# Last output product of a Strassen-form encoder layer: its weights loaded earlier and split earlier, its row statistics begun earlier

## Chip, cores and metric

The kernel runs on one core of a Trainium2 chip. The metric is device time in microseconds (us). The kernel before has a median of 2124.32 us over three runs (2120.95 to 2125.03).

## The reference

One layer of a hybrid encoder on a sequence of 1024 rows and 2048 columns. Attention and pooling branches give `merged` (1024 x 2048). The part that the change touches is the end:

```python
    merged = g_a * (y_a @ w_br_attn) + g_p * (y_p @ w_br_pool)
    o = merged @ w_out
    return x + gate[:, None] * rmsnorm(o, post_g)
```

`rmsnorm` divides each row of `o` by the root of the mean of its squares, so a row of the output can be written only when all 2048 columns of `o` in that row are known. Everything is in 32-bit floats.

## The kernel before

**Arithmetic.** A product of 32-bit floats is made from two reduced-precision parts: `split` (L95) copies a tile into a high part on ScalarE (L96, `hi`) and subtracts it from the source on VectorE (L97, `lo`). Three matmuls (hi by hi, lo by hi, hi by lo; L1351 to L1353 in the output stage) stand for one. The large products use the Strassen-Winograd scheme: seven block products in place of eight, of sums and differences of blocks. The sums of blocks of `w_out` (S1 to S4) are computed earlier in the program and lie in DRAM as `ws_d`; the blocks themselves (A11, A12, A22) are read from `w_out`.

**The output stage.** `out_pair(half, i, ...)` computes, for one half of the rows in each Strassen block and one half of the columns in each block, four result blocks. It runs four times; the last call (half 1, i 1) is called the final pair here. A call makes seven products in this order, each of 8 steps `j` for two row tiles `t`, that is 48 matmuls into PSUM banks X, Z or V. They are numbered 1 to 7 here; the code counts them from 0 (`n`):

1. A11 by B11 into X, which is then copied to Z
2. S3 by T3 into V, copied to `p7`
3. S2 by T2 added to Z, copied to `u2`
4. A12 by B21 added to X, which gives result block 11 (`c11`)
5. A22 by T4 added to V, with `u2` gives block 21
6. S1 by T1 added to Z, copied to `u4`, with `p7` gives block 22
7. S4 by B22 added to Z, which gives block 12 (`c12`)

`split_weights` (L1399) loads the raw weights of a product in four transfers of 512 KB (tag `raw`, ring of four buffers, tile name `wr`) and splits them step by step into a ring of four `whi` and four `wlo`. `between(n, jp)` is called after every second step of product n+1 and issues side work: for the final pair it is `between_11` (L1564). The prepared operands (B11, T3, ... B22, tiles `mh` and `ml`) fill the pool `big`, a ring of 56 slots of 256 KB; a new tile takes the slots in the order in which they were first given, so it must wait until the matmuls that read the old operand are done.

**Product 7 of the final pair** is written apart (L1470 to L1493). In the kernel before its weights are split ahead into 16 slots of `big` (`ring=False`), but the raw tiles come through the same ring of four as all the others, so their four transfers of 512 KB are issued behind those of product 6. Product 7 runs all 24 matmuls of row tile t=0 first and then those of t=1.

**Rows and their scale.** `result` (L1436) squares a block on ScalarE and sums along the row into `ssq[:, T, n]` (L1361), and multiplies it by the gain `g` on VectorE (L1441). `row_scale` (L1363) sums the four numbers (L1365), takes the root on ScalarE (L1366) and the reciprocal (L1367). `finish_block` (L1370) computes `r * scale + x` on VectorE (L1372) and stores it; the rows of x come as tiles `xr` (`fetch_x_block`, 256 KB each, into slots of `big`). Row tiles T=4 and 5 are finished by `third_block` (after product 5 they have all they need), row tile 6 after the t=0 half of product 7, and row tile 7 after the t=1 half.

**What sets the order.** Every engine executes its own list in order. A scheduler places the instructions in these lists; `keep` (L91) pins an instruction where the program puts it. All loads and the last stores go through SyncE's (SP's) list and its one queue; the stores of the first rows go through GpSimd's (POOL's).

Of the kernel before, what the change touches and what calls it, by code (L numbers as in the profile page):

```python
# [13 lines left out]
F32 = mybir.dt.float32  # L14
F32R = mybir.dt.float32r
AF = mybir.ActivationFunctionType
ALU = mybir.AluOpType
AX = mybir.AxisListType
# [3 lines left out]
P = 128  # L22
S = 1024
D = 2048
# [7 lines left out]
EPS = 1e-6  # L32
# [11 lines left out]
def encoder_layer(ctx: ExitStack, tc: tile.TileContext, x, c, table, w_ada, b_ada, pre_g,  # L44
# [15 lines left out]
    nc = tc.nc  # L60
# [5 lines left out]
    def pool(name, bufs=1, **kw):  # L66
        return tc.tile_pool(name=name, bufs=bufs, reuse_waits="tile", **kw)

    const = ctx.enter_context(pool("const"))
    big = ctx.enter_context(pool("big", 56))  # L70
    wp = ctx.enter_context(pool("wpool"))
# [5 lines left out]
    def uid(s):  # L77
        cnt[0] += 1
        return f"{s}_{cnt[0]}"
# [4 lines left out]
    def slot(name, dt=F32R, shape=(P, 512)):  # L84
        return big.tile(list(shape), dt, tag="big", name=uid(name))

    def f32(ap):
        return ap.bitcast(F32)


    def keep(ins):  # L91

        tc.keep_in_program_order(ins)

    def split(hi, lo, src, pin=False):  # L95
        ins = (nc.scalar.activation(hi, src, AF.Copy),  # L96
               nc.vector.tensor_tensor(lo, src, f32(hi), ALU.subtract))  # L97
        if pin:
            keep(ins[0])
            keep(ins[1])  # L100

    def add(o, a, b, eng=None):
        return (eng or nc.vector).tensor_tensor(o, a, b, ALU.add)  # L103
# [4 lines left out]
    load = nc.sync.dma_start  # L108
# [15 lines left out]
    JP = KT // 4  # L124
# [20 lines left out]
    def new_op(n=4):  # L145
        return {m: [None] * n for m in MOVING}
# [209 lines left out]
    for r0, src in ((0, c[0]), (16, b_ada[0, 0:D]), (32, b_ada[0, D:2 * D]),  # L356
                    (48, pre_g[0]), (64, b_merge[0]), (96, pool_scale[0])):
        n = src.shape[0] // P
# [180 lines left out]
    op = new_op()  # L539
# [196 lines left out]
    for tag in SEEDED:  # L736
        hi = op["B11"][0][0]
# [47 lines left out]
    def ws_rows(name):  # L785
        return ws_d[name].rearrange("(j p) n -> p j n", p=P)
# [166 lines left out]
    op = new_op()  # L953
# [270 lines left out]
    ssq = const.tile([P, NB, 4], F32, name="ssq_o")  # L1224
# [16 lines left out]
    for b, w in enumerate((w_ba, w_bp)):  # L1241
        op = new_op()
# [105 lines left out]
    def out_mm(pb, op, name, j, t, w, first, last):  # L1348
        ts_ = slice(t * P, (t + 1) * P)
        hi, lo = (o_[:, j % 2, ts_] for o_ in op[name][j // 2])  # L1350
        nc.tensor.matmul(pb, hi, w[0], start=first, stop=False, skip_group_check=True)  # L1351
        nc.tensor.matmul(pb, lo, w[0], start=False, stop=False, skip_group_check=True)  # L1352
        nc.tensor.matmul(pb, hi, w[1], start=False, stop=last, skip_group_check=True)  # L1353
# [3 lines left out]
    def rows_of(T, n):  # L1357
        return out[T * P:(T + 1) * P, n * 512:(n + 1) * 512]

    def square(src, T, n):  # L1360
        nc.scalar.activation(bank("at", "junk"), src, AF.Square, accum_out=ssq[:, T, n:n + 1])  # L1361

    def row_scale(T):  # L1363
        s_ = const.tile([P, 3], F32, tag="st", name=uid("st"), bufs=4)
        nc.vector.tensor_reduce(s_[:, 0:1], ssq[:, T], op=ALU.add, axis=AX.X)  # L1365
        nc.scalar.activation(s_[:, 1:2], s_[:, 0:1], AF.Sqrt, bias=eps_t, scale=1.0 / D)  # L1366
        nc.vector.reciprocal(s_[:, 2:3], s_[:, 1:2])  # L1367
        return s_[:, 2:3]

    def finish_block(T, n, scale, store=store):  # L1370
        r = held.pop((T, n))
        keep(nc.vector.scalar_tensor_tensor(r, r, scale, xrow.pop((T, n)), op0=ALU.mult, op1=ALU.add))  # L1372
        store(rows_of(T, n), r)
# [7 lines left out]
        return m[:, 0], m[:, 1]  # L1381

    first_raws = []

    def out_pair(half, i, op, between, after=None):


        final = half == 1 and i == 1
        stays = half == 1 or i == 1
        count = iter(range(7))  # L1390
        g = {}

        def fetch_gain():
            for nh in range(2):
                g[nh] = ev.tile([P, 512], F32, tag="ev", name=uid("pg"))
                n0 = nh * (D // 2) + i * 512
                load(g[nh], pg_d[0:1, n0:n0 + 512].to_broadcast([P, 512]))

        def split_weights(wname, ring=True, pin=()):  # L1399
            for jp in range(JP):  # L1400
                raw = first_raws.pop(0) if wname == "A11" and first_raws else weights(wname, i, jp)
                for jj in range(2):
                    hi, lo = (wp.tile([P, 512], F32R, tag=t, name=uid(t), bufs=4) if ring else slot(t)
                              for t in ("whi", "wlo"))
                    split(hi, lo, raw[:, jj], 2 * jp + jj in pin)
                    yield hi, lo


        def product(wname, mov, pbs, fresh=False):

            ws = split_weights(wname)
            n, nj = next(count), 2 * JP
            for j in range(nj - 2):
                w = next(ws)
                for t in range(2):
                    out_mm(pbs[t], op, mov, j, t, w, fresh and j == 0, False)
                if j % 2:
                    between(n, j // 2)
            w = list(ws)
            if n == 6:  # L1420
                first_raws.extend(weights("A11", 1 - i, jp) for jp in range(JP))
            for t in range(2):
                for j in (nj - 2, nj - 1):
                    out_mm(pbs[t], op, mov, j, t, w[j - nj + 2], False, j == nj - 1)
            between(n, JP - 1)

        def tiles(name):
            tag, bufs = {"p7": ("gt", 4), "u2": ("gt", 4), "c11": ("ev", 4), "u4": ("pv", 2)}[name]
            return [ev.tile([P, 512], F32, tag=tag, name=uid(name), bufs=bufs) for _ in range(2)]

        def copies(ts, pbs):
            for t in range(2):
                nc.scalar.activation(ts[t], pbs[t], AF.Copy)
            return ts

        def result(blk, t, src, dst):  # L1436

            T, nh = half * 4 + (int(blk[1]) - 1) * 2 + t, int(blk[0]) - 1
            n = 2 * nh + i
            square(src, T, n)  # L1440
            nc.vector.tensor_tensor(dst, src, g[nh], ALU.mult)  # L1441
            if stays:
                held[T, n] = dst
            else:
                nc.gpsimd.dma_start(o_d[T * P:(T + 1) * P, n * 512:(n + 1) * 512], dst)

        def kept(tag):

            return list(row_tiles()) if half == 1 and i == 0 else tiles(tag)

        bx, bz, bv = ([bank(tag, b) for tag in tags] for b, tags in
                      (("X", ("mm", "mm")), ("Z", SEEDED), ("V", ("sc", "sc"))))
        product("A11", "B11", bx, True)
        fetch_gain()
        for t in range(2):
            nc.scalar.activation(bz[t], bx[t], AF.Copy)
        product("S3", "T3", bv, True)
        p7 = copies(kept("p7"), bv)
        product("S2", "T2", bz)
        u2 = copies(kept("u2"), bz)  # L1460
        product("A12", "B21", bx)
        c11 = kept("c11")
        for t in range(2):
            result("11", t, bx[t], c11[t])
        product("A22", "T4", bv)
        for t in range(2):
            add(u2[t], bv[t], u2[t])
            result("21", t, u2[t], u2[t])
        product("S1", "T1", bz)
        if final:  # L1470
            last = split_weights("S4", ring=False, pin=(6, 7))
            ws = [next(last) for _ in range(6)]
        u4 = copies([slot("u4", F32) for _ in range(2)] if final else tiles("u4"), bz)
        if final:
            ws += list(last)
        for t in range(2):
            add(p7[t], p7[t], u4[t])
            result("22", t, p7[t], p7[t])
        if not final:
            product("S4", "B22", bz)  # L1480
            c12 = kept("u4")
            for t in range(2):
                result("12", t, bz[t], c12[t])
            return
        after()
        c12 = [slot("c12", F32) for _ in range(2)]
        for t in range(2):
            for j, w in enumerate(ws):
                out_mm(bz[t], op, "B22", j, t, w, False, j == len(ws) - 1)
            result("12", t, bz[t], c12[t])  # L1490
            scale = row_scale(6 + t)
            for n in (0, 2, 3, 1):
                finish_block(6 + t, n, scale)  # L1493

# [4 lines left out]
    ring = deque()  # L1499
# [64 lines left out]
    def between_11(n, jp):  # L1564
        if jp % 2 and n < 3:
            steps(1)
        if jp == JP - 1 and n in (2, 4):
            for T in (4, 5) if n == 2 else (6, 7):
                for b in range(4):
                    fetch_x_block(T, b, lambda name: slot(name, F32))  # L1570
# [50 lines left out]
```

## Time and profile before

| | |
|---|---|
| three timed runs | 2125.03, 2124.32, 2120.95 us |
| the profiled execution, as timed | 2121.29 us |
| its span, first to last instruction | 2119.5 us |
| granted TensorE clock over the span | 0.996 |
| busy: TensorE matmul (PE), VectorE (DVE), ScalarE (ACT) | 98%, 73%, 52% |
| queue of SyncE: bytes, share of 16 DMA engines' span | 457.82 MB, 66.3% |

The profiled execution is 1.8 us longer than its span: that lies around the first and the last instruction. A row of a timeline has start, duration (both us), engine, line, operation, output and inputs (buffer numbers left out), shape and count; in brackets stands how long the engine was idle before it and what ended that. A row of the windows view has a stretch, its length, the busy time and count of PE, PEld (weight loads), DVE, ACT and POOL, the granted clock, the mean busy share of the DMA engines and the rate in GB/s.

### The profile page before, as it was taken

What the parts mean: (1) busy time and instruction counts of PE and PEld (TensorE: products, weight loads), DVE (VectorE), ACT (ScalarE), POOL (GpSimd) and SP (SyncE); (2) the same over time, 40 slices, a digit from 0 to 9 for tenths busy, and PEclk for the clock granted to TensorE, in tenths of its full rate; (3) what the DMA queues carried; (4) which work ended last, traced back from release to release, by engine and by line L of the source; (5) the groups of instructions that cost most, each with busy time, mean ns of one, the idle gap of its engine ahead of it and who ended that gap; (6) DMA issues with size and microseconds to landing.
All of it is one profiled execution on the core that took longest, in us unless ns stands there. A gap on an engine that the chain in (4) does not pass through costs nothing.

```text
span 2119.5 us, 29008 instructions
## 1 busy us (share of the span) xinstructions
PE 2084.7 (98%) x9573; PEld 1717.4 (81%) x9573; DVE 1542.6 (73%) x2767; ACT 1108.7 (52%) x2106; POOL 20.1 (1%) x90
## 2 busy tenths in 40 slices
PE   6999999999999999999999999999999999999998
PEld 4688888888888888888888888888888788888886
DVE  5787666777546776677777688956957977889667
ACT  4654444444366544666666544333645644767654
POOL 0000000000000000000000000000000000000000
PEclk9999999999999999999999999999999999999999
DMA  9887666899757456544545477766745566686996
GB/s 328 273 264 234 196 198 206 286 312 322 259 191 240 146 178 202 174 157 159 191 156 162 158 238 229 221 213 197 244 159 168 180 195 198 219 311 216 299 335 223
DMA packets 302934, 468.20 MB, mean 221 GB/s; under 512 B 24074, under 2 KB 145058, under 8 KB 302784
## 3 DMA queue, kind: packets, MB, share of 16 engines
q1 hardware_dynamic: 299408, 457.82, 66.3%
q0 software_dynamic: 3040, 8.48, 1.0%
q8 instruction: 75, 1.23, 0.2%
q14 instruction: 75, 0.61, 0.1%
q10 hardware_dynamic: 336, 0.06, 0.0%
HBM read 341.45 MB, written 126.90 MB: 221 GB/s over the span
## 4 chain that ended last, share of the span: by engine, by line
PE 91%; DVE 4%; DMA 3%; ACT 1%; issue 1%; SPq 0%; ACTq 0%; DVEq 0%
PE Z L238 31%; PE X L238 21%; PE V L238 21%; PE Z L1351 2%; PE Z L1353 2%; PE Z L1352 2%; PE V L1351 1%; PE V L1353 1%; PE V L1352 1%; PE X L1353 1%; PE X L1351 1%; PE X L1352 1%; PE PT L1062 1%; DMA xt<-in_x_dram 1%; DMA wr<-ws_dS 1%
## 5 line engine op out<-in xcount | busy, mean ns | idle before, releaser
L96 ACT ACTIVATE whi<-raw 128x512 fp32r<-128x512 f32 (+1 forms) x532 | 322.1, 606 | 521.7 <-PE Z L238 242.0
L97 DVE TENSOR_TENSOR wlo<-raw,whi 128x512 fp32r<-128x512 f32 (+1 forms) x532 | 347.3, 657 | 172.6 <-PE Z L238 127.4
L97 DVE TENSOR_TENSOR wlo<-wr,whi 128x512 fp32r<-128x512 f32 x224 | 150.9, 689 | 56.8 <-ACT whi L96 48.3
L96 ACT ACTIVATE whi<-wr 128x512 fp32r<-128x512 f32 x224 | 138.4, 629 | 90.5 <-DVE wlo L97 36.0
L103 DVE TENSOR_TENSOR raw<-raw,raw 128x512 f32<-128x512 f32 x79 | 54.5, 690 | 97.6 <-DMA raw<-in_w_merge_dram 75.3
L238 PE MATMUL X<-B11h,whi 128*128 128x512 f32 x334 | 91.4, 392 | 2.4 <-ACT c L663 2.4
L96 ACT ACTIVATE whi<-ws 128x512 fp32r<-128x512 f32 (+1 forms) x88 | 53.5, 608 | 76.8 <-PE X L238 65.4
L238 PE MATMUL Z<-T2h,whi 128*128 128x512 f32 x334 | 91.2, 392 | 0.5 <-ACT whi L96 0.5
L238 PE MATMUL V<-T3h,whi 128*128 128x512 f32 x334 | 91.5, 393 | 0.0
L238 PE MATMUL Z<-T1h,whi 128*128 128x512 f32 x334 | 91.3, 391 | 0.0
L238 PE MATMUL Z<-B22h,whi 128*128 128x512 f32 x334 | 91.1, 392 | 0.0
L238 PE MATMUL Z<-T2h,wlo 128*128 128x512 f32 x334 | 90.3, 390 | 0.6 <-DVE wlo L97 0.6
L238 PE MATMUL X<-B21h,whi 128*128 128x512 f32 x334 | 90.8, 391 | 0.0
L238 PE MATMUL X<-B11h,wlo 128*128 128x512 f32 x334 | 90.7, 391 | 0.0
L238 PE MATMUL V<-T3l,whi 128*128 128x512 f32 x334 | 90.6, 391 | 0.0
L238 PE MATMUL V<-T4h,whi 128*128 128x512 f32 x334 | 90.6, 391 | 0.0
L238 PE MATMUL V<-T4l,whi 128*128 128x512 f32 x334 | 90.5, 390 | 0.1
L238 PE MATMUL V<-T3h,wlo 128*128 128x512 f32 x334 | 90.5, 391 | 0.0
L238 PE MATMUL X<-B11l,whi 128*128 128x512 f32 x334 | 90.5, 390 | 0.0
L238 PE MATMUL Z<-T1l,whi 128*128 128x512 f32 x334 | 90.4, 390 | 0.1
L238 PE MATMUL Z<-T1h,wlo 128*128 128x512 f32 x334 | 90.3, 390 | 0.0
L238 PE MATMUL Z<-B22l,whi 128*128 128x512 f32 x334 | 90.2, 390 | 0.0
(353 smaller groups left out, 4839.6 us busy)
## 6 DMA issues: line engine op xcount, KB each, us to landing
part<-part_d SPq DMA_DIRECT2D x136, 256.0 KB, 4.7
ada<-in_w_ada_dram SPq DMA_DIRECT2D x128, 256.0 KB, 5.2
raw<-in_w_merge_dram SPq DMA_DIRECT2D x64, 512.0 KB, 5.8
wr<-ws_dS SPq DMA_DIRECT2D x64, 512.0 KB, 5.1
raw<-in_w_in_dram SPq DMA_DIRECT2D x62, 512.0 KB, 4.1
wr<-in_w_out_dram SPq DMA_DIRECT2D x48, 512.0 KB, 5.2
proj_d<-part SPq DMA_DIRECT2D x68, 256.0 KB, 2.3
sw<-in_w_out_dram SPq DMA_DIRECT2D x64, 256.0 KB, 5.9
```

Source lines behind the costliest of these rows:

```text
L96: ins = (nc.scalar.activation(hi, src, AF.Copy), nc.vector.tensor_tensor(lo, src, f32(hi), ALU.subtract))
L97: nc.vector.tensor_tensor(lo, src, f32(hi), ALU.subtract))
L103: return (eng or nc.vector).tensor_tensor(o, a, b, ALU.add)
L238: nc.tensor.matmul(ps, w_[:, i], op[mov][j][m_], start=fresh and i == 0 and n == 0, stop=i == nj - 1 and n == 2, skip_group_check=True)
L1062: nc.tensor.transpose(pt[:, i * P:(i + 1) * P], p[:, i * P:(i + 1) * P], ident)
L1351: nc.tensor.matmul(pb, hi, w[0], start=first, stop=False, skip_group_check=True)
L1352: nc.tensor.matmul(pb, lo, w[0], start=False, stop=False, skip_group_check=True)
L1353: nc.tensor.matmul(pb, hi, w[1], start=False, stop=last, skip_group_check=True)
```

## The change

Three things change, all in the final pair.

1. The raw weights of product 7 are loaded as eight transfers of 256 KB (`fetch_last_weight`), two after every second step of product 3, into eight slots of `big`: the first ones of the ring, those of operand B11. They are pinned.
2. They are split (`split_last_weight`, pinned) one step after every second step of product 4 (j 0 to 3) and of product 5 (j 4 to 7), into 16 slots of `big`. The four loads of 512 KB and the splits around product 6 go away. The slots that the rows of x take are others now, and the rows for T=6 and 7 are asked for after product 6 (n == 5) and no longer after product 5.
3. For row tiles 6 and 7, `row_scale` becomes two parts. `rest_of_row` sums the squares of three blocks and forms the mean and EPS from them, before the last matmuls. `scale_of` takes the fourth sum as the input of the root and the rest as its bias.

```diff
+    def rest_of_row(T):
+        s_ = const.tile([P, 3], F32, tag="st", name=uid("st"), bufs=4)
+        nc.vector.tensor_reduce(s_[:, 1:2], ssq[:, T, 2:4], op=ALU.add, axis=AX.X)
+        add(s_[:, 1:2], s_[:, 1:2], ssq[:, T, 0:1])
+        nc.vector.tensor_scalar(s_[:, 0:1], s_[:, 1:2], 1.0 / D, EPS, op0=ALU.mult, op1=ALU.add)
+        return s_
+
+    def scale_of(T, s_):
+        nc.scalar.activation(s_[:, 1:2], ssq[:, T, 1:2], AF.Sqrt, bias=s_[:, 0:1], scale=1.0 / D)
+        nc.vector.reciprocal(s_[:, 2:3], s_[:, 1:2])
+        return s_[:, 2:3]
...
+    last_raws, last_weights = [], []
+
+    def fetch_last_weight(j):
+        last_raws.append(slot("wr", F32))
+        keep(load(last_raws[j], ws_rows("S4")[:, j, 512:1024]))
+
+    def split_last_weight(j):
+        last_weights.append((slot("whi"), slot("wlo")))
+        split(*last_weights[j], last_raws[j], True)
...
-        if final:
-            last = split_weights("S4", ring=False, pin=(6, 7))
-            ws = [next(last) for _ in range(6)]
         u4 = copies([slot("u4", F32) for _ in range(2)] if final else tiles("u4"), bz)
-        if final:
-            ws += list(last)
...
         c12 = [slot("c12", F32) for _ in range(2)]
+        rest = [rest_of_row(6 + t) for t in range(2)]
         for t in range(2):
-            for j, w in enumerate(ws):
-                out_mm(bz[t], op, "B22", j, t, w, False, j == len(ws) - 1)
+            for j, w in enumerate(last_weights):
+                out_mm(bz[t], op, "B22", j, t, w, False, j == len(last_weights) - 1)
             result("12", t, bz[t], c12[t])
-            scale = row_scale(6 + t)
+            scale = scale_of(6 + t, rest[t])
...
-        if jp == JP - 1 and n in (2, 4):
+        if n == 2:
+            fetch_last_weight(2 * jp)
+            fetch_last_weight(2 * jp + 1)
+        if n in (3, 4):
+            split_last_weight(4 * (n - 3) + jp)
+        if jp == JP - 1 and n in (2, 5):
             for T in (4, 5) if n == 2 else (6, 7):
```

**SyncE's list, from the first weights of product 3 on.** Names are tile, numbers, source; `wr` with `128x2x512` is 512 KB, `128x512` is 256 KB. Before, from the first load for product 3 (S2) to the first load for product 4 (`in_w_out`, A12):

```order
L1342 DMA wr_4135_19590<-ws_dS2_97 128x2x512
L1377 DMA xr_4159_19686<-in_x_dram 128x512
L1342 DMA wr_4140_19612<-ws_dS2_97 128x2x512
L1377 DMA xr_4160_19688<-in_x_dram 128x512
L1377 DMA xr_4161_19690<-in_x_dram 128x512
L1342 DMA wr_4145_19634<-ws_dS2_97 128x2x512
L1377 DMA xr_4162_19692<-in_x_dram 128x512
L1342 DMA wr_4150_19656<-ws_dS2_97 128x2x512
L1377 DMA xr_4209_19882<-in_x_dram 128x512
L1345 DMA wr_4165_19698<-in_w_out_dram 128x2x512
```

In the changed kernel, first the loads between those for product 3:

```order
L1342 DMA wr_4135_19590<-ws_dS2_97 128x2x512
L1400 DMA wr_4140_19612<-ws_dS4_99 128x512
L1400 DMA wr_4141_19614<-ws_dS4_99 128x512
L1342 DMA wr_4142_19616<-ws_dS2_97 128x2x512
L1400 DMA wr_4147_19638<-ws_dS4_99 128x512
L1400 DMA wr_4148_19640<-ws_dS4_99 128x512
L1342 DMA wr_4149_19642<-ws_dS2_97 128x2x512
L1400 DMA wr_4154_19664<-ws_dS4_99 128x512
L1400 DMA wr_4155_19666<-ws_dS4_99 128x512
L1342 DMA wr_4156_19668<-ws_dS2_97 128x2x512
```

and right behind them, up to the first load for product 4:

```order
L1400 DMA wr_4161_19690<-ws_dS4_99 128x512
L1400 DMA wr_4162_19692<-ws_dS4_99 128x512
L1389 DMA xr_4163_19694<-in_x_dram 128x512
L1389 DMA xr_4164_19696<-in_x_dram 128x512
L1389 DMA xr_4165_19698<-in_x_dram 128x512
L1389 DMA xr_4166_19700<-in_x_dram 128x512
L1389 DMA xr_4167_19702<-in_x_dram 128x512
L1389 DMA xr_4168_19704<-in_x_dram 128x512
L1389 DMA xr_4169_19706<-in_x_dram 128x512
L1389 DMA xr_4170_19708<-in_x_dram 128x512
L1345 DMA wr_4173_19714<-in_w_out_dram 128x2x512
```

Before, four loads of x rows stood earlier, among those for product 2, and five stand here: nine of 256 KB in all ahead of the first A12 load, counted from product 2's first two loads. Now there are sixteen, eight of S4 and eight of x rows. Behind that A12 load stood seven loads of x rows, among those of A12 and A22; now eight stand behind it (T=6 and 7), around and after the last load of S1.

**TensorE's list, start of product 4.** `whi_4174`/`wlo_4175` are the parts of A12's first step, X_4089 and X_4090 the banks of t=0 and t=1. In the changed kernel, from the product's second matmul to its sixth:

```order
 L1352 MATMUL X_4089_19394<-whi_4174_19716,ml_3819_18317 128x512
 L1351 MATMUL X_4090_19395<-whi_4174_19716,mh_3818_18316 128x512
 L1353 MATMUL X_4089_19394<-wlo_4175_19717,mh_3818_18316 128x512
 L1352 MATMUL X_4090_19395<-whi_4174_19716,ml_3819_18317 128x512
 L1353 MATMUL X_4090_19395<-wlo_4175_19717,mh_3818_18316 128x512
```

The first matmul that reads the low part stands fourth in the product now; before it stood third, ahead of the first one into X_4090. Otherwise TensorE's list is the same.

**VectorE's list, end of the program.** `p7` is block 22, `c12` block 12, `st` the row statistics. Before, the last twelve instructions up to the statistics of row tile 6:

```order
L103 TENSOR_TENSOR p7_4134_19587<-p7_4134_19587,u4_4255_20025 128x512
L97 TENSOR_TENSOR wlo_4258_20031<-wr_4256_20028,whi_4257_20030 128x512
L1441 TENSOR_TENSOR p7_4133_19586<-p7_4133_19586,pg_4112_19490 128x512
L97 TENSOR_TENSOR wlo_4260_20035<-wr_4256_20028,whi_4259_20034 128x512
L1441 TENSOR_TENSOR p7_4134_19587<-p7_4134_19587,pg_4112_19490 128x512
L1372 TENSOR_SCALAR u2_4163_19694<-u2_4163_19694,st_4263_20046,xr_4158_19684 128x512
L1372 TENSOR_SCALAR mo_4013_19064<-mo_4013_19064,st_4264_20058,xr_4159_19686 128x512
L1372 TENSOR_SCALAR c11_4186_19787<-c11_4186_19787,st_4264_20058,xr_4160_19688 128x512
L1372 TENSOR_SCALAR mo_3992_18967<-mo_3992_18967,st_4264_20058,xr_4161_19690 128x512
L1372 TENSOR_SCALAR u2_4164_19695<-u2_4164_19695,st_4264_20058,xr_4162_19692 128x512
L1441 TENSOR_TENSOR c12_4265_20070<-Z_4091_19396,pg_4111_19488 128x512
L1365 TENSOR_REDUCE st_4268_20099<-ssq_o_14169 128x1
```

In the changed kernel:

```order
L103 TENSOR_TENSOR p7_4133_19586<-p7_4133_19586,u4_4263_20042 128x512
L1384 TENSOR_SCALAR u2_4172_19711<-u2_4172_19711,st_4268_20066,xr_4170_19708 128x512
L103 TENSOR_TENSOR p7_4134_19587<-p7_4134_19587,u4_4264_20043 128x512
L1461 TENSOR_TENSOR p7_4133_19586<-p7_4133_19586,pg_4112_19490 128x512
L1372 TENSOR_REDUCE st_4271_20080<-ssq_o_14169 128x1
L103 TENSOR_TENSOR st_4271_20080<-st_4271_20080,ssq_o_14169 128x1
L1461 TENSOR_TENSOR p7_4134_19587<-p7_4134_19587,pg_4112_19490 128x512
L1374 TENSOR_SCALAR st_4271_20080<-st_4271_20080 128x1
L1372 TENSOR_REDUCE st_4272_20084<-ssq_o_14169 128x1
L103 TENSOR_TENSOR st_4272_20084<-st_4272_20084,ssq_o_14169 128x1
L1374 TENSOR_SCALAR st_4272_20084<-st_4272_20084 128x1
L1461 TENSOR_TENSOR c12_4269_20078<-Z_4091_19396,pg_4111_19488 128x512
```

The splits of S4 are gone from here, seven of the eight blocks of `third_block` stand ahead of the work on `p7` and the eighth within it, and the row statistics stand ahead of the `c12` work. Behind the last row each block 12 is followed by the reciprocal alone, with the root on ScalarE between them.

More of the change, by code (lines that the diff above doesn't have):

```diff
@@ L1397, in fetch_gain, with split_weights @@
                 load(g[nh], pg_d[0:1, n0:n0 + 512].to_broadcast([P, 512]))
-        def split_weights(wname, ring=True, pin=()):
+        def split_weights(wname):
             for jp in range(JP):
@@ L1402, in split_weights @@
                 for jj in range(2):
-                    hi, lo = (wp.tile([P, 512], F32R, tag=t, name=uid(t), bufs=4) if ring else slot(t)
-                              for t in ("whi", "wlo"))
-                    split(hi, lo, raw[:, jj], 2 * jp + jj in pin)
+                    hi, lo = (wp.tile([P, 512], F32R, tag=t, name=uid(t), bufs=4) for t in ("whi", "wlo"))
+                    split(hi, lo, raw[:, jj])
                     yield hi, lo
```

## The prediction

> **What bounds the kernel now.** I read the page, then the windows of the final pair's products, then the chain, then the last rows of VectorE and ScalarE.
>
> ```profile
> span 2119.5 us, 29008 instructions
> PE 2084.7 (98%) x9573; PEld 1717.4 (81%) x9573; DVE 1542.6 (73%) x2767; ACT 1108.7 (52%) x2106; POOL 20.1 (1%) x90
> ```
>
> TensorE is busy for 98% of the span. Up to the final pair both programs are the same, so only the stretch from 2033 us on can change. Its products 2 to 7, one row each (PE, PEld, DVE, ACT, POOL, clock, DMA share, GB/s):
>
> ```profile
> 2045.13:2056.04 10.91, 10.91 (x49) 8.75 (x47) 7.40 (x12) 6.86 (x14) 1.08 (x2) 1.00 1.05 393
> 2056.04:2066.92 10.88, 10.88 (x50) 9.01 (x48) 5.28 (x9) 5.81 (x12) 0.00 (x0) 1.00 1.05 382
> 2066.92:2077.90 10.98, 10.98 (x50) 9.11 (x49) 6.03 (x9) 6.14 (x12) 0.00 (x0) 1.00 0.83 298
> 2077.90:2088.80 10.90, 10.90 (x50) 9.03 (x49) 6.91 (x12) 5.73 (x11) 0.00 (x0) 1.00 0.57 193
> 2088.80:2099.70 10.90, 10.90 (x50) 8.98 (x49) 10.03 (x21) 8.18 (x18) 0.00 (x0) 1.00 0.62 204
> 2099.70:2110.60 10.90, 10.90 (x49) 8.69 (x47) 10.50 (x20) 4.07 (x10) 0.00 (x0) 1.00 0.50 181
> ```
>
> TensorE never pauses in these 65 us. So splitting product 7's weights earlier cannot shorten them: product 7 already starts at once. Two things can: what follows TensorE's last matmul gets shorter, or a load comes too late and TensorE waits. The DMA columns say where: in products 2 and 3 the engines are full (share 1.05), and that is where the change puts its loads. From product 5 on, from where it takes loads away, they are little over half used.
>
> The end of the program, VectorE and ScalarE:
>
> ```profile
> 2107.21 0.75 DVE L1372 SCALAR_TENSOR_TENSOR u<-u,st,xr 128x512 f32<-128x512 f32 x1
> ...
> 2111.18 0.75 DVE L1372 SCALAR_TENSOR_TENSOR c<-c,st,xr 128x512 f32<-128x512 f32 x1
> 2111.84 0.69 DVE L1441 TENSOR_TENSOR c<-Z,pg 128x512 f32<-128x512 f32 x1
> 2112.44 0.15 DVE L1365 TENSOR_REDUCE st<-ssq_o 128x1 f32<-128x4 f32 x1
> 2112.95 0.16 DVE L1367 RECIPROCAL st<-st 128x1 f32<-128x1 f32 x1 [0.36 <-ACT st L1366]
> 2113.15 1.41 DVE L1372 SCALAR_TENSOR_TENSOR mo<-mo,st,xr 128x512 f32<-128x512 f32 x2
> ```
>
> ```profile
> 2105.29 0.58 ACT L1361 ACTIVATE junk<-Z 128x512 f32<-128x512 f32 x1 [1.76 <-PE Z L1353]
> ...
> 2110.73 0.58 ACT L1361 ACTIVATE junk<-Z 128x512 f32<-128x512 f32 x1 [1.78 <-PE Z L1353]
> 2111.22 0.19 ACT L1361 ACTIVATION_READ_ACCUMULATOR junk<-Z 128x1 f32 x1
> 2112.62 0.29 ACT L1366 ACTIVATE st<-st,eps_t 128x1 f32<-128x1 f32 x1 [1.21 <-DVE st L1365]
> ```
>
> TensorE is done near 2110.6, the last square's sum at 2111.22 + 0.19 = 2111.41, yet the last multiply by the gain starts only at 2111.84, because VectorE still works through its backlog (row at 2111.18). Then reduce, root and reciprocal follow one another, and the first block of row tile 7 starts at 2113.15.
>
> **The shorter end.** The multiply waits for the square's sum, as this pair shows for product 4:
>
> ```profile
> 2077.13 0.19 ACT L1361 ACTIVATION_READ_ACCUMULATOR junk<-X 128x1 f32 x1
> ```
>
> ```profile
> 2077.36 0.69 DVE L1441 TENSOR_TENSOR c<-X,pg 128x512 f32<-128x512 f32 x1 [0.95 <-ACT junk L1361]
> ```
>
> It starts 0.04 us after the sum (2077.13 + 0.19 to 2077.36). A VectorE without backlog thus starts the last multiply at 2111.45: **0.39 us** gained. Behind it stood reduce, root and reciprocal, 2113.15 - 2111.84 = 1.31 us from multiply to first block. Now only the reciprocal stands there: 0.60 us for the multiply (2111.84 to 2112.44) and 0.20 for the reciprocal (2112.95 to 2113.15), 0.80 in all: **0.51 us** gained. The root (0.29) needs the sum alone and ends near 2111.74, beside the multiply. The rest (four blocks, last store) stays as it is. Together -0.90 us.
>
> That needs the backlog gone. After product 6 VectorE has to do two additions and two multiplies for p7 (0.60 each), one block (2111.84 - 2111.18 = 0.66) and six statistics of at most 0.15: 4.0 us from about 2100.4, when the copy of Z by ScalarE is there, so until 2104.4. The other seven blocks, 4.6 us, fit ahead of that: product 6's last split waits for the buffer of its fourth step, free at 2088.80 + 4 x 10.9 / 8 = 2094.3, and with 0.69 us each on ScalarE and VectorE is done by 2095.7. The multiply of row tile 6 comes 0.72 us after the square at 2105.29; from there 0.80 + 4 x 0.66 lead to 2109.5, before 2111.45. The four instructions that the statistics add cost nothing in that idle time. Without it the 0.90 is lost; below that they can cost 0.6 (four of 0.15).
>
> **The splits beside products 4 and 5.** Four more in each: on ScalarE and VectorE at most 0.69 us each (the shape of the multiply at 2111.84), 2.8 us on top of 6.0 to 6.9 us of 10.9. They are covered by idle time; if in front of a needed split, one delays it by 0.7 us, once. I take zero. The fewer instructions in products 6 and 7 gain nothing beyond the end above.
>
> **The loads.** This is the term that decides. Transfers of SyncE's queue, rows of its timeline, of its DMA view over 2046 to 2066 us, and the landing of the first A12 load:
>
> ```profile
> 2054.72 0.38 SPq L1345 DMA_DIRECT2D wr<-in_w_out_dram  x1
> ```
>
> ```profile
> DMA packets 3963, 7.77 MB, mean 388 GB/s; under 512 B 353, under 2 KB 353, under 8 KB 3961
> ```
>
> ```profile
> L1345 SPq DMA_DIRECT2D wr<-in_w_out_dram x1: 378/378/378, 2054.7 to 2054.7; - x1
> ...
> DMA to landing us min/median/max: 8.4/8.4/8.4
> ```
>
> The load is issued at 2054.72 and lands at 2063.1. At 388 GB/s a transfer of 262,144 bytes takes 0.68 us, so 8.4 us are mostly queue. By the lists nine transfers of 256 KB stood ahead of it since the engines filled up; now sixteen. Seven more are 7 x 0.676 = 4.7 us: it lands at 2067.8. TensorE begins product 4 at 2066.92 (window row). What TensorE loses when a first load is late is seen at product 2:
>
> ```profile
> 2035.31 8.64 DMA wr<-ws_dS
> 2044.06 0.64 ACT whi L96
> 2044.75 0.50 PE V L1351
> ```
>
> ```profile
> 2044.75 0.50 PE L1351 MATMUL V<-whi,mh 128*128 128x512 f32 x1
> 2045.08 0.40 PE L1352 MATMUL V<-whi,ml 128*128 128x512 f32 x1
> 2045.47 0.50 PE L1353 MATMUL V<-wlo,mh 128*128 128x512 f32 x1
> ```
>
> The load lands at 2043.95 and the first matmul starts 0.80 later, with 0.33 to the second in place of the usual 0.23 (10.9 / 48). The matmul that needs the low part could start 1.52 after landing; as the fourth, where the new list has it, it is due at 0.80 + 0.33 + 0.46 = 1.59, so it waits no more. Loss: 2067.8 + 0.80 + 0.10 - 2066.92 = **1.8 us**. The second A12 load, of 512 KB, lands 2 x 0.68 = 1.4 us after the first and is needed 12 matmuls, 2.7 us, after it, so it adds no wait; ScalarE and VectorE have 10.9 - 6.1 - 2.8 = 2.0 us to spare in product 4 to catch up. Product 5's first load is issued when A12's first splits free its buffer, 9 us or more ahead of its use, and even a full queue landed it within 8.4.
>
> Bounds: zero, if the late load shares the engines with those ahead and does not queue behind all of them. Above: if SyncE holds the last x rows until product 2 has freed their slots (2056.04), the A12 load is issued up to 2.1 us later (2056.8), 3.9 us lost. I take 1.8, as 8.4 us of landing at full engines is nearest to a queue in order. The Trainium skill, page "DMA: Bandwidth & Descriptors", section "Where 436 GB/s comes from", says that HBM binds at about 358 GB/s for one core; the row above moved 388, so the measurement decides. At 358 the seven would take 5.1 us and the sum would be 0.4 us higher.
>
> **Sum.** 2121.29 (2119.5 of span and 1.8 around it) + 1.8 - 0.9 = 2122.2. The profiled execution is 3.0 us under the median; the four executions (2125.03, 2124.32, 2120.95, 2121.29) have a mean of 2122.9. With +0.9 I say **2123.8**. It is no change: 0.2% is 4.2 us, about what a measurement of this kernel can tell from none.
>
> **Rivals.**
> - *No wait*: the A12 load lands in time. For it: TensorE's products 3 to 7 have not waited once. Against: the 8.4 us of queue. -0.9: 2122.0.
> - *The clock falls in the wait* (slower). Early in the program TensorE idled, and then ran at half clock:
>
> ```profile
> 68.80:72.20 3.40, 1.02 (x5) 0.82 (x5) 2.95 (x7) 2.75 (x7) 0.00 (x0) 1.00 1.10 348
> 72.20:75.60 3.40, 3.40 (x10) 2.67 (x9) 0.43 (x1) 1.84 (x4) 0.00 (x0) 0.50 1.10 348
> ...
> 642.00:646.00 4.00, 2.80 (x15) 2.08 (x14) 1.52 (x3) 2.47 (x8) 0.00 (x0) 1.00 0.99 358
> ```
>
>  With 2.4 us idle in 3.4 the clock fell to 0.50 for 3.4 us; with 1.2 idle in 4.0 it stayed at 1.00. My wait is 1.7 us, between them. Half the work of 3.4 us is lost: +1.7, thus +2.6 in all, 2125.5; it decides somewhere between 1.2 and 2.4 us of idling. With the upper bound of the wait, 3.9, it is 3.9 + 1.7 - 0.9 = +4.7, 2127.6. The Trainium skill, page "TensorE: Matmul & The Clock Gate", section "Part 1: The HAM clock gate (the "warmup" mystery)", puts the fall after a whole idle window of about 3.4 us; by that rule 1.7 us would not do it, though the first row fell with 1.02 us busy.
> - *The end is not shortened* (the change does not do what it says): something other than the backlog holds the last multiply. Against: the pair at 2077. +1.8: 2124.7.
>
> **How the numbers follow.** Forecast 0.55, no wait 0.2, clock 0.15, end not shortened 0.1. The executions lie 2 us around their mean, so the range goes from 2122.0 - 2.1 = 2119.9 to 2125.5 + 2.1 = 2127.6. Faster by over 0.2% (under 2120.1 against the median) only in the low tail of *no wait*: 0.07. Slower (over 2128.6): the clock case with the long wait and some tails: 0.12. Within: 0.81.
>
> **What would show it.** Right: an idle TensorE of 1 to 2 us at the start of product 4, put down to ScalarE's `whi` and the load of A12; landing of that load over 10 us after product 3's last one was issued, with full DMA engines from 2046 to 2068; idle VectorE before both block-12 multiplies; 0.8 us from the last multiply to the first block of row tile 7. Wrong: a wait in products 5 to 7, a granted clock under 1.00 near 2070, or VectorE busy without a gap when TensorE ends.

## The result

The changed kernel takes 2126.7 us (median of 17 runs, 2124.15 to 2131.41) beside 2122.7 us for the kernel before on the same chip (17 runs, 2119.32 to 2126.95): a ratio of 1.002, 95% interval 1.0013 to 1.0027. That is **4.0 us slower** (2.8 to 5.7). The forecast was +0.9, called no change. The place of the loss and its sign were right; its size was not.

The profiled execution of the changed kernel took 2125.27 us, with a span of 2123.5 us at a mean clock of 0.996. The windows of products 1 to 4, with TensorE's idle stretch as a row of its own (PE, PEld, DVE, ACT, POOL, clock, DMA share, GB/s):

```profile
2035.79:2046.67 10.88, 10.88 (x49) 9.01 (x48) 6.47 (x11) 4.82 (x11) 1.08 (x2) 1.00 0.92 296
2046.67:2057.57 10.90, 10.90 (x49) 8.94 (x48) 7.49 (x13) 7.03 (x14) 1.08 (x2) 1.00 0.99 324
2057.57:2068.61 11.04, 11.04 (x49) 8.82 (x47) 3.92 (x6) 4.00 (x7) 0.00 (x0) 1.00 1.04 371
2068.61:2071.95 3.34, 0.01 (x2) 0.01 (x1) 0.02 (x1) 0.69 (x2) 0.00 (x0) 1.00 1.04 390
2071.95:2082.99 11.04, 11.04 (x48) 9.04 (x49) 9.79 (x16) 9.22 (x19) 0.00 (x0) 1.00 0.83 268
```

TensorE stands still for 3.34 us while the DMA engines are full. What it waits for stands in the timelines of TensorE, of ScalarE and in the source view of SyncE's A12 load:

```profile
2071.95 0.50 PE L1351 MATMUL X<-whi,mh 128*128 128x512 f32 x1 [3.33 <-ACT whi L96]
```

```profile
2071.26 1.15 ACT L96 ACTIVATE whi<-wr 128x512 fp32r<-128x512 f32 x2 [3.38 <-DMA wr<-in_w_out_dram]
```

```profile
L1345 SPq DMA_DIRECT2D wr<-in_w_out_dram x1: 385/385/385, 2065.7 to 2065.7; - x1
...
DMA to landing us min/median/max: 5.5/5.5/5.5
```

The load of A12 is issued at 2065.7 and lands at 2071.2; 0.8 us later product 4 starts. A product without a wait takes 10.88 us, so it was due at 2057.57 + 10.88 = 2068.45: 3.50 us are lost there, and 0.16 in product 4 (11.04). The last rows of VectorE and ScalarE:

```profile
2113.96 0.74 DVE L1384 SCALAR_TENSOR_TENSOR c<-c,st,xr 128x512 f32<-128x512 f32 x1
2116.55 0.69 DVE L1461 TENSOR_TENSOR c<-Z,pg 128x512 f32<-128x512 f32 x1 [1.84 <-ACT junk L1361]
2117.16 0.15 DVE L1379 RECIPROCAL st<-st 128x1 f32<-128x1 f32 x1
2117.34 1.41 DVE L1384 SCALAR_TENSOR_TENSOR mo<-mo,st,xr 128x512 f32<-128x512 f32 x2
```

```profile
2115.83 0.58 ACT L1361 ACTIVATE junk<-Z 128x512 f32<-128x512 f32 x1 [4.36 <-PE Z L1353]
2116.32 0.19 ACT L1361 ACTIVATION_READ_ACCUMULATOR junk<-Z 128x1 f32 x1
2116.55 0.29 ACT L1378 ACTIVATE st<-ssq_o,st 128x1 f32<-128x1 f32 x1
```

VectorE is idle for 1.84 us before the last multiply, root and multiply run side by side, and from the last square to the first block of row tile 7 it is 2117.34 - 2115.83 = 1.51 us; before it was 2113.15 - 2110.73 = 2.42. The end is shorter by 0.91 us.

Product 3 starts 1.5 us later than in the profile of before (2057.57 and 2056.04). Two profiles of the same changed kernel differ by more (2057.57 and 2059.93), but the two kernels with the old loads are the earliest of all profiles here (2056.04 and 2056.11), so the profiles by themselves do not rule out a loss ahead of product 3. The timed runs of the kernel with the x rows later do, below. From the start of product 3 to the end it is 63.5 us before (2119.5 - 2056.04) and 65.9 after: +2.5 in these two executions.

### The profile page after: what moved, and what is told of

Its sections match the earlier page's. It is cut to its first block, busy times and chain, and to the rows that moved or that the text cites. A ratio compares the mean times of both kernels' runs of the same rounds, so it can differ in the third digit from the quotient of the medians.

```text
span 2123.5 us, 29016 instructions
## 1 busy us (share of the span) xinstructions
PE 2087.0 (98%) x9573; PEld 1717.9 (81%) x9573; DVE 1542.6 (73%) x2771; ACT 1108.7 (52%) x2106; POOL 20.2 (1%) x90
## 4 chain that ended last, share of the span: by engine, by line
PE 87%; DMA 6%; DVE 4%; ACT 1%; issue 1%; SPq 0%; DVEq 0%; ACTq 0%; POOL 0%; POOLq 0%
PE Z L238 29%; PE X L238 19%; PE V L238 19%; PE Z L1351 2%; PE Z L1352 2%; PE Z L1353 2%; DMA xt<-in_x_dram 1%; DMA raw<-in_w_merge_dram 1%; PE X L1351 1%; PE X L1352 1%; PE V L1352 1%; PE X L1353 1%; PE V L1351 1%; PE V L1353 1%; PE PT L1062 1%
```

## The experiments

Theory after the result: the transfers ahead of A12's first load make it late, each by its own time at full engines. Rivals: the splits or the shortened end cost the time; SyncE's list is held up by the pinned loads; the difference comes from ahead of the final pair; the clock falls. All ratios are to the kernel before on the same chip.

**The end alone.** The kernel before with part 3 of the change and nothing else:

```
+        rest = [rest_of_row(6 + t) for t in range(2)]
...
-            scale = row_scale(6 + t)
+            scale = scale_of(6 + t, rest[t])
```

> The kernel before with the third part of the change alone: the statistics of row tiles 6 and 7 split into a part ahead and a root with bias; loads and splits as before. Queue theory (the loss of the change is the late A12 load, its gain the short end): no wait of TensorE at product 4; from the last square's start to the first block of row tile 7 at most 2.0 us (2.4 before, 1.5 in the changed kernel), since the backlog of VectorE stays but the reduce is gone; time 0.3 to 0.9 us under before, not to be told from it by the median. Rival (the changed kernel is slower upstream of the final pair, by its layout): no statement, since nothing upstream differs here.

Ratio 0.9997 (0.9988 to 1.0005). VectorE's last rows:

```profile
2111.56 0.75 DVE L1384 SCALAR_TENSOR_TENSOR c<-c,st,xr 128x512 f32<-128x512 f32 x1
2112.22 0.68 DVE L1453 TENSOR_TENSOR c<-Z,pg 128x512 f32<-128x512 f32 x1
2112.82 0.15 DVE L1379 RECIPROCAL st<-st 128x1 f32<-128x1 f32 x1
2113.01 1.42 DVE L1384 SCALAR_TENSOR_TENSOR mo<-mo,st,xr 128x512 f32<-128x512 f32 x2
```

The expectation for the gap failed: from the last square (2110.71) to the first block it is 2.30 us, not at most 2.0. Multiply to block is 0.79 us, as in the changed kernel, but the multiply itself starts only at 2112.22, behind the blocks of row tile 6. Without the earlier splits the four new statistics lengthen the very backlog that holds the multiply, so the two parts of the end are worth 0.9 only together.

**The loads and splits alone.** The changed kernel with the old `row_scale` (parts 1 and 2):

```
-        rest = [rest_of_row(6 + t) for t in range(2)]
...
-            scale = scale_of(6 + t, rest[t])
+            scale = row_scale(6 + t)
```

> The changed kernel with the old row statistics (one reduce, root, reciprocal after the last square): loads and splits moved, end not shortened but without VectorE's backlog. Queue theory: TensorE idles 3 to 3.6 us at the start of product 4, as in the changed kernel; from the last square to the first block of row tile 7 about 2.0 us (0.5 more than in the changed kernel); time 0.5 us over the changed kernel. Rival (clock): the idle time is the same, and in this execution the granted clock falls to 0.5 for 3.4 us behind it, 1.7 us more.

Ratio 1.0015 (1.0007 to 1.0023): the loss is with the loads and splits, not with the end. The windows of product 3 and product 4:

```profile
2058.83:2069.87 11.04, 11.04 (x49) 8.82 (x47) 3.91 (x6) 3.99 (x7) 0.00 (x0) 1.00 1.05 373
2073.43:2086.03 12.60, 12.60 (x48) 10.28 (x49) 10.08 (x16) 9.43 (x19) 0.00 (x0) 0.86 0.67 226
```

Product 4 was due at 2058.83 + 10.88 = 2069.71 and starts 3.72 later. It also takes 12.60 in place of 10.88, at a mean clock of 0.86. This execution has something that the profile of the changed kernel lacks: the clock fell. At the end VectorE is idle for 1.38 us before the last multiply, and the first block follows the last square by 2.04 us (2118.93 to 2120.97) in place of 2.42: the earlier splits by themselves give 0.4 of the 0.9.

**The x rows behind the A12 loads.** Eight transfers of 256 KB leave the place ahead of A12; the loads of product 7's weights stay as in the change:

```
-        if jp == JP - 1 and n in (2, 5):
-            for T in (4, 5) if n == 2 else (6, 7):
+        if jp == JP - 1 and n in (3, 5):
+            for T in (4, 5) if n == 3 else (6, 7):
```

> The changed kernel with the eight loads of x rows for T=4 and 5 asked for after product 4 and no longer after product 3, so that they stand behind the loads of A12; the eight loads of S4 stay where they are. Queue theory: eight transfers of 256 KB fewer ahead of the first A12 load, 5.4 us, more than the 3.3 us of idling, so no wait at product 4; from the first matmul of the final pair to the end 83.5 to 85 us (85.9 before, 87.7 in the changed kernel); time 1 to 2.5 us under before. Rival (SyncE is held by the pinned loads of S4): the wait stays at 3 us or falls only to 2. Rival (upstream): still 2 us over before.

Ratio **0.999 (0.9981 to 0.9998)**, 2120.97 us: faster than the kernel before, by little more than the noise. Windows of products 3 and 4, and the A12 load:

```profile
2057.04:2067.92 10.88, 10.88 (x50) 9.01 (x48) 5.40 (x9) 5.55 (x11) 0.00 (x0) 1.00 1.04 371
2067.92:2078.80 10.88, 10.88 (x50) 9.01 (x48) 8.09 (x13) 7.94 (x17) 0.00 (x0) 1.00 0.76 252
```

```profile
L1345 SPq DMA_DIRECT2D wr<-in_w_out_dram x1: 384/384/384, 2056.4 to 2056.4; - x1
...
DMA to landing us min/median/max: 9.3/9.3/9.3
```

It lands at 2065.7, 2.2 us before product 4 is due, and nothing waits. Three rivals fall with it: the splits cost nothing there (products 4 and 5 have them still and take 10.88 us each), the pinned loads do not hold SyncE up, and a loss ahead of the final pair would be here too, since the program ahead of it is the same as in the change.

**The weights one product earlier.** Product 7's weights asked for during product 2, all else as in the change:

```
-        if n == 2:
+        if n == 1:
             fetch_last_weight(2 * jp)
```

> The changed kernel with the eight loads of S4 asked for one product earlier, two after every second step of product 2: they then use the time in products 1 and 2 in which the queue has room (262 GB/s in product 1 of the changed kernel, 289 before, against 390 when full). x rows as in the changed kernel. Queue theory: the same bytes ahead of A12, but begun earlier; the idle time at product 4 falls from 3.3 us to 1 to 2 us, the value that the prediction had; a small wait in product 2 (its last weights now stand behind six transfers) is possible. Time 1 to 2.5 us under the changed kernel. Rival (only the number of transfers ahead of the load counts, whenever they are issued): 3.3 us as in the changed kernel.

Ratio 1.0005 (0.9996 to 1.0013). Windows of products 2 to 4:

```profile
2044.41:2056.30 11.89, 11.86 (x49) 8.59 (x47) 6.29 (x11) 5.38 (x11) 1.08 (x2) 1.00 1.04 395
2056.30:2067.75 11.45, 11.45 (x49) 8.85 (x48) 5.34 (x8) 4.90 (x9) 0.00 (x0) 1.00 0.98 352
2069.37:2082.28 12.91, 12.91 (x48) 10.17 (x49) 10.16 (x16) 9.91 (x20) 0.00 (x0) 0.87 0.58 188
```

Product 2 moves 395 GB/s here and 324 in the changed kernel: the room that the change leaves unused in product 2 is filled, and TensorE idles 1.62 us at product 4 (2067.75 to 2069.37) in place of 3.33, as the queue theory had it; that only the number of transfers counts, whenever they are asked for, falls. But the loads for products 2 and 3 come late now: product 2 takes 1.0 us longer. And the clock fell in product 4 after only 1.62 us of idling.

**The weights one product later.** Loads during product 4, splits beside products 5 and 6:

```
-        if n == 2:
+        if n == 3:
             fetch_last_weight(2 * jp)
...
-        if n in (3, 4):
-            split_last_weight(4 * (n - 3) + jp)
+        if n in (4, 5):
+            split_last_weight(4 * (n - 4) + jp)
```

> The changed kernel with the weights of product 7 asked for during product 4 in place of product 3 and split beside products 5 and 6 in place of 4 and 5. SyncE's list then has A12's first load ahead of all eight of them, with five x rows behind product 3's first load, as in the kernel before. Theory (sixteen transfers that stand ahead of A12's first load make TensorE wait): no idle time at product 4, so the shortened end of 0.9 us is kept, last multiply to first block 0.8, ratio 0.9996 to 0.9980, as for the run with the x rows moved back. Rival (the splits or the loads themselves cost time, wherever they stand): TensorE idles at product 4, 5 or 7 for over 1 us, ratio over 1.000. Second rival (half of product 7's weights come too late when split beside product 6, which leaves VectorE a backlog at the end as before): TensorE does not idle, but the gap from the last square to the first block is 2.0 to 2.4 in place of 1.5.

Ratio **0.9989 (0.998 to 0.9998)**, 2121.57 us. Windows of products 3 and 4, and the A12 load:

```profile
core 0 of [0], span 2121.0 us
...
2058.79:2069.67 10.88, 10.88 (x49) 9.01 (x48) 5.36 (x9) 6.00 (x12) 0.00 (x0) 1.00 1.05 390
2069.67:2080.55 10.88, 10.88 (x49) 9.01 (x48) 6.53 (x10) 6.56 (x13) 0.00 (x0) 1.00 0.87 309
```

```profile
L1345 SPq DMA_DIRECT2D wr<-in_w_out_dram x1: 379/379/379, 2057.6 to 2057.6; - x1
...
DMA to landing us min/median/max: 7.1/7.1/7.1
```

It lands at 2064.7, 5.0 us ahead. No wait, and the gap from last square to first block stays at 1.52 us (2113.39 to 2114.91), so the second rival (a backlog again) falls too. From product 3 to the end it is 2121.0 - 2058.79 = 62.2 us, 1.25 less than before (63.46), of which the end explains 0.9.

**Half of the x rows.** Four behind the A12 loads, four ahead:

```
-        if jp == JP - 1 and n in (2, 5):
-            for T in (4, 5) if n == 2 else (6, 7):
+        if jp == JP - 1 and n in (2, 3, 5):
+            for T in {2: (4,), 3: (5,), 5: (6, 7)}[n]:
```

> The changed kernel with only the four x rows of T=4 ahead of A12's first load and the four of T=5 behind product 4's loads. Theory (each transfer of 256 KB ahead of A12 costs its time at full engines, 0.68 us): four fewer take 2.7 us off the idle 3.3 us: TensorE idles 0.6 us (0.3 to 1.0) at product 4, and the ratio lies between that of the changed kernel (1.002) and that of the run with all eight moved (0.999), near 1.000. Rival (any room left on the queue puts the load in time, or the wait hangs on the last x row's slot): no idle time at all. Clock rival (TensorE's clock falls after any idle time there): clock 0.5 for 3.4 us, 1.7 us lost in product 4 on top.

Ratio 0.9996 (0.9987 to 1.0005). Windows of products 3 and 4, and the A12 load:

```profile
2057.15:2068.19 11.04, 11.04 (x49) 8.82 (x47) 3.88 (x6) 3.74 (x8) 0.00 (x0) 1.00 1.02 366
2068.70:2079.98 11.28, 11.28 (x49) 9.04 (x49) 9.88 (x16) 9.71 (x20) 0.00 (x0) 1.00 0.74 240
```

```profile
L1345 SPq DMA_DIRECT2D wr<-in_w_out_dram x1: 384/384/384, 2061.6 to 2061.6; - x1
...
DMA to landing us min/median/max: 6.3/6.3/6.3
```

TensorE idles 0.51 us (2068.19 to 2068.70). Product 4 starts 0.67 after it is due (2068.03) and takes 0.40 longer than 10.88, so 1.1 us are lost, against 0.9 gained at the end. The theory gave 0.6 for the idle time. The rival "any room on the queue is enough" falls. The clock stayed at 1.00.

**The changed kernel once more.** One execution, 2130.04 us.

> The changed kernel once more, one execution, for the clock alone. If the granted clock falls after a wait of 3.3 to 3.6 us in some executions only, as it did with the end of before (fell) and did not in the profile of the changed kernel, then idle time of 3.3 to 3.6 us at product 4 again, with product 4 either 11.0 us long (clock stays) or 12.6 (clock falls). The execution may show either; the wait itself should be there in both.

```profile
2059.93:2070.97 11.04, 11.04 (x49) 8.82 (x47) 3.98 (x6) 4.51 (x8) 0.00 (x0) 1.00 1.05 374
2075.14:2087.77 12.63, 12.63 (x49) 10.24 (x49) 10.08 (x16) 9.44 (x19) 0.00 (x0) 0.86 0.64 202
```

TensorE idles 4.17 us here, more than the 3.3 to 3.6 that I had expected, and product 4 took 12.63 us: the clock fell. So the changed kernel itself does both.

**The x rows on another queue.** The same eight x rows through GpSimd's queue:

```
-                    fetch_x_block(T, b, lambda name: slot(name, F32))
+                    if T < 6:
+                        xrow[T, b] = slot("xr", F32)
+                        keep(nc.gpsimd.dma_start(xrow[T, b], x[T * P:(T + 1) * P, b * 512:(b + 1) * 512]))
+                        continue
+                    fetch_x_block(T, b, lambda name: slot(name, F32))
```

> The changed kernel with the eight x rows of T=4 and 5 asked for on GpSimd's queue in place of SyncE's, at the same place of the program. SyncE's list then has eight transfers fewer ahead of A12's first load, as in the run with the rows moved back, but the bytes are still moved in the same stretch. Theory A (place in SyncE's queue and its eight outstanding transfers decide): A12's first load is issued near 2056 and lands near 2066, no idle time at product 4, ratio 0.998 to 1.000. Theory B (bytes decide, since all queues share 16 engines): it lands up to 5.4 us later than that, TensorE idles 1 to 3 us, ratio 1.0005 to 1.002.

Ratio 1.002 (1.001 to 1.003): theory B, and worse than it said. The source view of the last load of product 3's weights (S2), and TensorE's timeline in product 3:

```profile
L1342 SPq DMA_DIRECT2D wr<-ws_dS x1: 662/662/662, 2055.8 to 2055.8; - x1
...
DMA to landing us min/median/max: 14.7/14.7/14.7
```

```profile
2067.44 0.39 PE L1353 MATMUL Z<-wlo,mh 128*128 128x512 f32 x1
2071.23 0.80 PE L1351 MATMUL Z<-whi,mh 128*128 128x512 f32 x1 [3.40 <-ACT whi L96]
```

The engines were full already, so now even the load ahead of A12's is late and the wait of 3.40 us stands in product 3. With both queues the engines moved 363 GB/s (2059.51 to 2066.91, share 1.04), no more than the 371 of the changed kernel's product 3. The same S2 load lands after 9.6 us in the changed kernel, issued at 2053.5; here A12's first load is issued at 2060.0, 5.7 us earlier than there, and still lands only 14.7 us later, at 2074.7, where theory A had 2066. What delays a load is the bytes that move at the same time, not its place in SyncE's list alone. The clock fell as well, to 0.50 from 2070.32 to 2077.15, and is part of this ratio.

**All together.** How long before product 4 is due (start of product 3 + 10.88) the first A12 load has landed, against the transfers of 256 KB that stand between product 3's first load and A12's in the list, product 3's own left out:

| kernel | transfers ahead | due | landed | to spare |
|---|---|---|---|---|
| weights later | 4 | 2069.67 | 2064.7 | 5.0 |
| before | 5 | 2066.92 | 2063.1 | 3.8 |
| end alone (2055.0 + 8.4) | 5 | 2066.99 | 2063.4 | 3.6 |
| x rows later | 8 | 2067.92 | 2065.7 | 2.2 |
| half of the x rows | 12 | 2068.03 | 2067.9 | 0.1 |
| changed | 16 | 2068.45 | 2071.2 | -2.8 |
| loads and splits alone (2066.7 + 6.0) | 16 | 2069.71 | 2072.7 | -3.0 |
| changed, once more (2067.9 + 6.4) | 16 | 2070.81 | 2074.3 | -3.5 |
| weights one product earlier (2061.1 + 7.5) | 8 | 2067.18 | 2068.6 | -1.4 |

```profile
L1345 SPq DMA_DIRECT2D wr<-in_w_out_dram x1: 386/386/386, 2067.9 to 2067.9; - x1
...
DMA to landing us min/median/max: 6.4/6.4/6.4
```

From the first row to those with sixteen, twelve more transfers cost 7.8 to 8.5 us, 0.65 to 0.71 each, about the 0.68 that one takes at full engines. The steps between are less even: 1.2 us for the one from four to five, 0.5 each from five to twelve, 0.7 to 0.9 each from twelve to sixteen. TensorE needs 0.8 to spare (the first split), and waits below that.

The last row does not fit, for the count starts at product 3's first load, and there that load is late itself: it lands at 2055.5, 0.8 us before product 3 starts (2056.30), where before it is 3.5 and in the changed kernel 4.8. Counted from the landing of that load to the landing of A12's, it comes near: 13.1 us, beside 14.4 with the x rows later, both with eight. The same count gives 10.6 us before (2052.5 to 2063.1) and 18.4 in the changed kernel (2052.8 to 2071.2): 7.8 us for eleven transfers, 0.71 each.

**The clock.** These rows cut the time before product 4 at the edges at which the clock can change: the changed kernel (stays), the changed kernel once more and the weights one product earlier (fall). In the last two the edges are those of the fall itself. In the first the edge is worked out from the fall at 2118.27, after the last matmul: in the other two such a fall comes 47.79 us behind the one in product 4 (2075.82 to 2123.61 and 2070.96 to 2118.75), 14 stretches of 3.41 us, and 47.79 us before 2118.27 lies 2070.48.

```profile
2067.07:2070.48 3.41, 1.54 (x7) 0.94 (x5) 0.00 (x0) 0.60 (x1) 0.00 (x0) 1.00 1.01 361
2070.48:2073.90 3.42, 1.96 (x8) 1.53 (x9) 1.74 (x3) 2.64 (x6) 0.00 (x0) 1.00 1.02 380
...
2118.27:2121.68 3.41, 0.00 (x0) 0.00 (x0) 1.81 (x3) 0.00 (x0) 0.00 (x0) 0.50 0.83 298
```

```profile
2069.00:2072.41 3.41, 1.97 (x9) 1.31 (x7) 0.00 (x0) 0.60 (x1) 0.00 (x0) 1.00 1.02 363
2072.41:2075.82 3.41, 0.68 (x3) 0.48 (x3) 0.70 (x2) 1.36 (x3) 0.00 (x0) 1.00 1.04 389
2075.82:2079.23 3.41, 3.41 (x10) 2.71 (x9) 3.18 (x6) 2.87 (x6) 0.00 (x0) 0.50 0.53 174
```

```profile
2067.55:2070.96 3.41, 1.79 (x7) 1.02 (x7) 1.61 (x3) 2.28 (x5) 0.00 (x0) 1.00 0.79 291
2070.96:2074.37 3.41, 3.41 (x10) 2.63 (x9) 2.93 (x6) 3.16 (x7) 0.00 (x0) 0.50 0.54 175
```

In the changed kernel an edge at 2070.48 cuts the idle 3.33 us into 1.87 and 1.47, and the clock stays. In the third kernel 1.62 us lie within one stretch, and the clock falls. It is shown that a wait of 1.62 us can bring the fall and one of 3.33 us need not, and that the fall made product 4 1.7 us longer (12.60 and 12.63 in place of 10.88). That the place of the edges decides it fits the rows with 0.68 (fell) and with 1.96 and 1.97 (stayed); the 1.79 that fell and the 1.54 that stayed lie the wrong way round for a single threshold of busy time, so the exact rule stays open. Both have 7 matmuls in the stretch, where an undisturbed one has 3.41 / (10.88 / 48) = 15. The Trainium skill, page "TensorE: Matmul & The Clock Gate", section "Part 1: The HAM clock gate (the "warmup" mystery)", says that the gate watches a free-running window of 3.413 us; the length of the half-clock rows, 3.41 us, agrees. It puts the fall after at least one idle window; here a window with TensorE busy for 1.79 of 3.41 us sufficed.

## Why the prediction was wrong

**Right: the shorter end.** Forecast -0.90 us; measured -0.91, with VectorE idle before both block-12 multiplies (2.54 and 1.84 us). The condition, no backlog, was right as well: the end alone, with the backlog, gained 0.12. The splits beside products 4 and 5 were costed at nothing, and the kernel with the x rows later shows no loss in them.

**Right: where the loss arises.** TensorE waits for the first split of A12 at product 4, 0.8 us after landing; no other product of the final pair waits in its profile.

**Wrong, and it decides: the number of transfers.** The step that failed: "By the lists nine transfers of 256 KB stood ahead of it since the engines filled up; now sixteen. Seven more are 7 x 0.676 = 4.7 us". The price of one was right (0.65 to 0.71 measured), the count was not. It counted from product 2's first loads in both kernels, as if the engines were full from there on in both. The windows of products 1 and 2 of before say otherwise beside those of after:

```profile
2033.57:2044.45 10.88, 10.88 (x49) 8.82 (x47) 5.96 (x10) 4.02 (x9) 1.08 (x2) 1.00 0.90 289
2044.45:2056.04 11.59, 11.46 (x50) 9.05 (x49) 7.80 (x12) 7.54 (x15) 1.08 (x2) 1.00 1.05 393
```

Before, product 2 moves 393 GB/s, after 324: four of the x rows were asked for in product 1 (2036.5 to 2042.1), ahead of product 3's weights, and in the changed kernel nothing took their place, as the new loads stand behind product 3's first one. So not seven but eleven more transfers stand between product 3's first load and A12's (16 in place of 5): 11 x 0.676 = 7.4 us, of which 6.6 to 7.3 show in the table (3.8 + 2.8 and 3.8 + 3.5). Product 4 starts 3.5 and 4.3 us late in place of 1.8. The kernel with the weights one product earlier fills the room in product 2, and its idle time is 1.62 us, about the forecast's. That the measured loss lies near my upper bound of 3.9 is luck: that bound came from another reason (slots of x rows freed late by TensorE), and in the changed kernel's profile no load of x rows waits for TensorE; they wait for earlier loads to land.

**Wrong: the clock.** I gave "the clock falls in the wait" a chance of 0.15 because a wait of 1.7 us lay between a case that fell and one that did not. It was bound to the forecast's own wait, so the error above carried over: with 3.3 to 4.2 us the clock falls in some executions and stays in others. It fell after 1.62 us too, close to the forecast's own wait. The price, +1.7, was right (1.72 and 1.75 with the fall).

**The sum with the measured terms.** TensorE loses 3.50 + 0.16 in the changed kernel's profile, 4.33 + 1.75 in its second one and 3.72 + 1.72 with the loads and splits alone: 5.1 in the mean. Less 0.9 at the end, that gives +4.2, beside the 4.0 (2.8 to 5.7) of the timed runs. Three executions, one of them with the old end, do not fix how often the clock falls, so the close agreement is in part luck.

## What to carry to other kernels

Before moving loads ahead, count the bytes between the new place and the next load that someone waits for, from the last moment at which the engines had room, and compare with what that load has to spare; loads taken out of an earlier stretch do not help unless something moves up into it. Here 3.8 us to spare, less 0.8 for the split, at 0.68 for 256 KB, were room for four more transfers; the change added eleven. The same change gains 0.1%, barely clear of the noise (0.999, up to 0.9998), when other transfers step behind the urgent load, or when its own do.

## What the runs showed of the hardware

- Another queue was no way round full engines: with the eight x rows on GpSimd's queue the last load of product 3's weights took 14.7 us to land, where the same load took 9.6 in the changed kernel with one queue for all of them.
- The clock fell to 0.50 for one stretch of 3.41 us after TensorE had idled no more than 1.62 us, and stayed at 1.00 after 3.33 us in another execution.
